# Down projections of a two-layer trunk: ten of 22 k-blocks in seven block products instead of eight

## The chip, the core and the metric

The kernel runs on one core of a Trainium2 chip. Its time is the device time of one execution in microseconds (us). Five engines work side by side, each through its own instructions in order: PE (TensorE, the matrix products; PEld is its weight loads), DVE (VectorE), ACT (ScalarE), POOL (GpSimd) and SP (SyncE), of which the last two issue transfers here. An engine stands still where its next instruction waits for another engine or for a transfer, and everything queued behind that instruction waits with it.

## What is computed

The reference runs two layers over 512 positions of 1024 channels. Each layer is a token mixer with a residual, then a gated feed-forward block with a residual:

```
u, v = split(h @ w_up)               # 1024 -> 2 x 2816
u = causal_dwconv(u, conv_w, conv_b)
y = (gelu(u) * v) @ w_down           # 2816 -> 1024
x = x + y
```

The change concerns the last product, with `w_down`, once in each layer. Cut into blocks of 128, it has 22 blocks of the summed dimension (k-blocks) and 8 blocks of outputs, and 512 positions as the moving side.

## The kernel before

**Three passes.** Every float32 operand is split into a high part (ACT copies it to the reduced type, `hi`) and a low part (DVE subtracts, `lo`). A product is three matmuls: high by high, high by low, low by high (`accumulate`, matmul in line 266; `seven_product`, line 538). Moving operands are split too (`mh`, `ml` and others, by `split`, lines 179 and 180).

**Seven in place of eight.** A product of a 2 by 2 arrangement of weight blocks with a 2 by 2 arrangement of operand blocks has eight block products. The kernel does seven, on sums and differences of the blocks, named p1 to p7. The two sides of the arrangement are a pair of output blocks, two groups of k-blocks, and the two halves of 256 positions (`lo_t`, `hi_t`), so these matmuls have 256 columns where plain ones have 512.

**Down projections** (inside `ffn`, lines 691 to 893). Of the 22 k-blocks 14 are plain (`NPLAIN`), in two weight blocks of seven (`DOWN_K`), for each of eight output blocks. The other eight go through the seven products, in two groups of four (`HK`), for four pairs p of output blocks. `UNIT` is the planned time of twelve half-width matmuls, one of the seven products; `MM` is that of one plain matmul. The order on PE is: output blocks 0 to 3 plain; then pair 0, block 4 plain; pair 1, block 5; pair 2, block 6; pair 3, block 7. In layer 1 the last plain block is done as two halves of positions (`down_half`), so that the final norm of the first half can run beside the second. Two of the seven products accumulate straight onto the plain sums of an even output block; the rest is put together by `keep` (line 799, ACT), `add_p5` (802), `add_left` (818) and `add_right` (823), which with `add_x` update `x` (815, 816), and `finish` squares `x` for the next norm (square on ACT 293, sum on DVE 294).

**Weights of a pair** (`seven_weights`, line 456). SP loads one part twice (462), POOL adds another by a summing transfer (466), SP loads the left part (470) and the right part (474). ACT and DVE then form the sums s2 (495) and s4 (501) and the high and low parts of pieces a1, s31p, s2 and a2 (484, 490). Plain weight blocks come through `fetch_steps` (216 load, 221 high, 225 low). The loads of left part, right part and plain blocks share three buffers of 1024 columns (`wp`, tag raw): a load waits in SP's queue until the low part of an earlier one has been taken.

**Order.** Inside `ffn` each step is put down with a planned time (`at`), and PE, DVE and ACT run their steps exactly in order of these times. The times set the order and nothing else; an engine that is early runs on, one that is late is late. SP and POOL are placed by the scheduler.

**Operands of the seven products** (`mix_m`, line 700). From the eight last gated blocks DVE forms four sums of 256 columns each per k-pair (716 to 719), and ACT and DVE split them. These run while PE does the plain blocks 0 to 3.

**The end** (`last`, line 1477 on, layer 1). After the first half of positions has its norm, `scale_first` (1560) scales it in groups of two channel blocks on DVE and SP sends each out (1561); the second half is transposed on PE, normed and sent as `res` (1554). Which step follows which matmul is set by a counter of matmuls (`after(14, ...)`, `after(25, ...)`).

Buffers: `big` has 41 tiles of 512 columns (`NBIG`), eight PSUM banks hold sums, and software-issued transfers have descriptor space at the start of the on-chip memory.

Of the kernel before, what the change touches and what calls it, by code (L numbers as in the profile page):

```python
# [7 lines left out]
F32 = mybir.dt.float32  # L8
# [6 lines left out]
P = 128  # L15
# [17 lines left out]
WPITCH = WBLK + 64  # L33
SKEW = 19
VG_SKEW = 48
NBIG = 41
NSIDE = 8
AHEAD = 1
H = T // 2
# [13 lines left out]
DOWN_SEVEN = ("p1", "p2", "p6", "p5", "p7", "p3", "p4")  # L53
PE_AT_FIRST = {"p1": 0, "p2": 1, "p3": 2, "p6": 3, "p5": 4, "p7": 7, "p4": 9}
PE_AT_LAST = {"p1": 0, "p2": 1, "p6": 3, "p5": 5, "p7": 6, "p3": 7, "p4": 8}
NPLAIN = NF - KD
DOWN_K = (7, 7)
DOWN_AT = (0, 7)
NDOWN = 6

COLS = {}
# [10 lines left out]


@with_exitstack
def trunk_kernel(ctx, tc, xT, cols, w_first, w_lead, w_ab, w_pool, w_abo, w_vg, w_qk, w_r, w_g2, w_go, w_up, w_dn, w_ds, out):
    nc = tc.nc
    V, S, G, PE = nc.vector, nc.scalar, nc.gpsimd, nc.tensor

# [351 lines left out]
    def at(t, fn):  # L430
        events.append((t, len(events), fn))
# [24 lines left out]
    def seven_weights(src, base, pool, sums, behind=False, lead=None, later=0.0, begin=(26.0, 20.0, 15.4, 9.7), early=0.0):  # L456
# [57 lines left out]
        when = (-6.75, -4.35, -2.7, -2.4, -1.65, -0.95, -0.3, 1.55, 1.5, 3.3)  # L514
        if pool == "up":
            when = (*when[:7], *((2.2, 1.5, 4.4) if lead is not None else (0.4, 1.5, 3.3)))
        if pool == "gla":
            when = (-6.75, -4.35, -2.1, -1.6, -0.9, -0.2, 0.5, 4.4, 1.5, 5.3)
        if lead is not None and lead < 2:
# [5 lines left out]

        return w

    def seven_product(w, b, ops, name, out, first, ts, only=None, low_last=False):
        if out not in b:
            b[out] = bank("st" + out)  # L530
        piece, side = LEFT[name]
        ks = [slice(side * QUARTER + k * P, side * QUARTER + (k + 1) * P) for k in range(HK)]
        h, lo = w[piece]
        ah, al = ops[name]()
        for i in range(3) if only is None else (only,):
            wt, a = ((h, ah), (lo, ah), (h, al))[i] if low_last else ((h, ah), (h, al), (lo, ah))[i]
            for k in range(HK):
                PE.matmul(  # L538
                    b[out][:, ts], wt[:, ks[k]], a[k],
                    start=first and i == 0 and k == 0, stop=i == 2 and k == HK - 1,  # L540
                    skip_group_check=True,
                )

# [72 lines left out]
    def ffn(l, acc, mixed, finish, ahead, halves_last=False):  # L616
# [83 lines left out]
        def mix_m(i, t):  # L700
            def low_part():
                if i % 2 == 0:
                    mixed_m["b1", i // 2] = slot(F32R, "bh"), slot(F32R, "bl")
                h, lo = [b[:, i % 2 * H : i % 2 * H + H] for b in mixed_m["b1", i // 2]]
                mixed_m["p1", i] = h, lo
                split(h, lo, ms[NPLAIN + i][:, lo_t])

            def right_part():
                h, lo = slot(F32R, "bh"), slot(F32R, "bl")
                split(h, lo, ms[NPLAIN + HK + i])  # L710
                mixed_m["p2", i] = h[:, lo_t], lo[:, lo_t]
                mixed_m["p3", i] = h[:, hi_t], lo[:, hi_t]

            def sums():
                m1, m2 = ms[NPLAIN + i], ms[NPLAIN + HK + i]
                V.tensor_tensor(m1[:, lo_t], m1[:, lo_t], m1[:, hi_t], ALU.subtract)
                V.tensor_tensor(m1[:, hi_t], m2[:, hi_t], m1[:, hi_t], ALU.subtract)
                V.tensor_tensor(m2[:, hi_t], m1[:, lo_t], m2[:, hi_t], ALU.add)
                V.tensor_tensor(m2[:, lo_t], m2[:, hi_t], m2[:, lo_t], ALU.subtract)

            def ta_part():
                split(xh[i], xl[i], ms[NPLAIN + i])
                mixed_m["p5", i] = xh[i][:, lo_t], xl[i][:, lo_t]
                mixed_m["p7", i] = xh[i][:, hi_t], xl[i][:, hi_t]

            def tb_part():
                h, lo = xh[HK + i], xl[HK + i]
                split(h, lo, ms[NPLAIN + HK + i])
                mixed_m["p6", i] = h[:, hi_t], lo[:, hi_t]
                mixed_m["p4", i] = h[:, lo_t], lo[:, lo_t]  # L730

            at(t, low_part)
            at(t + 0.4, right_part)
            at(t + 1.1, sums)
            at(t + 3.4, ta_part)
            at(t + 4.0, tb_part)

# [12 lines left out]
            base += PAIR + NORM * (j == 1)  # L750
        base -= PAIR
        at(base + 5.6, lambda: open_stage("dn", NDOWN))
        for t in (5.8, 6.6, 8.0, 10.3, 10.9, 11.5, 12.2, 14.5, 15.2, 16.4, 17.6, 18.3, 19.0, 20.6):
            at(base + t, split_m)
        for i in range(HK):
            mix_m(i, base + 22.0 + 6.2 * i)

        o, late, ops = {}, {}, {}

# [19 lines left out]

        def down_seven(p, base):  # L780
            w = seven_weights(w_ds[l, p], base, "dn", 2)
            b, q = {}, {}

            def product(name):
                if not ops:
                    for n in LEFT:
                        ops[n] = lambda n=n: ([mixed_m[n, i][0] for i in k1], [mixed_m[n, i][1] for i in k1])
# [6 lines left out]
                seven_product(w, b, ops, name, out, first, ts)  # L794

            def keep(tile, ts):
                if tile not in q:
                    q[tile] = slot(name=tile)
                S.activation(q[tile][:, ts], b["x"][:, lo_t], AF.Copy)

            def add_p5(tile):
                V.tensor_tensor(q[tile][:, hi_t], b["z"][:, lo_t], q[tile][:, hi_t], ALU.add)

            for n, name in enumerate(DOWN_SEVEN):
                at(base + n * UNIT, lambda name=name: product(name))
            at(base + 1 * UNIT + 0.1, lambda: keep("kk", lo_t))
            at(base + 3 * UNIT + 0.1, lambda: keep("kk", hi_t))
            at(base + 4 * UNIT + 0.2, lambda: add_p5("kk"))
            at(base + 5 * UNIT + 0.1, lambda: keep("uu", hi_t))
            at(base + 5 * UNIT + 0.6, lambda: add_p5("uu"))  # L810
            at(base + 7 * UNIT + 0.1, lambda: keep("uu", lo_t))
            return q

        def add_x(j, out, ts=slice(0, T)):
# [20 lines left out]
        blocks = list(down_blocks())  # L835
        parts = {}

        def plain_down(j):
            nonlocal t
            while blocks and (blocks[0][0] == j or (j == 0 and blocks[0][0] < 4)):  # L840
                jj, k0, kt = blocks.pop(0)
                first = t < base + 9.5 * UNIT
                block(t - 16.0, t - (9.3 if first else 6.0), t - (7.0 if first else 4.5))
                if halves_last and jj == KD - 1:
                    at(t, lambda a=(0, k0, kt): down_half(*a))
                    t += 1.5 * kt * MM
                else:
                    at(t, lambda a=(jj, k0, kt): down(*a))
                    t += 3 * kt * MM

        def sevens(p):
            nonlocal t
            parts[p] = down_seven(p, t)
            t += 7 * UNIT

        def done_left(p):
            at(t + 0.3, lambda: add_left(p))
            at(t + 2.3, lambda: finish(2 * p))

        def done_right(p, t):  # L860
            at(t, lambda: add_right(p))
            at(t + 2.4, lambda: finish(2 * p + 1))

        plain_down(0)
        for p in range(HK):
            sevens(p)
            done_left(p)
            if p < HK - 1:
                done_right(p, t + 3 * NPLAIN * MM + 0.3)
            elif halves_last:  # L870
                at(t + 0.5, lambda: early_right(p))
            else:
                for j in range(KD - 2):
                    at(t + 0.5 + 1.5 * j, lambda j=j: pre_split(j, "mix1"))
            plain_down(HK + p)
        if halves_last:
            at(t, lambda: add_x(KD - 1, o["half"][:, :H], lo_t))
            at(t, lambda: finish(KD - 1, 0))
# [602 lines left out]
    def last(j, half=None):  # L1481
# [33 lines left out]
        if half == 0:  # L1515
            S.activation(x[j][:, ts], x[j][:, ts], AF.Copy, scale=col("fin", j))

            def both():
                part(0, acc[:, ts])
                part(1, sq)  # L1520
                root()

            def spread():
                tokens.append(spread_small(y2, 2))
                scale_first((0, 2, 4))

            after(14, both)
            after(25, spread)
            return
        xf = slot(name="xf")[:, :256]  # L1530
        V.tensor_scalar(xf, x[j][:, ts], col("fin", j), None, ALU.mult)
        scale_first((6,))
        to = [[bank("to") for e in range(2)] for c in range(2)]

        def turn(k):
# [106 lines left out]
```

## Time and profile before

| What | us |
|---|---|
| median of 3 runs (lowest, highest) | 1000.76 (1000.57, 1000.95) |
| profiled execution, its own time | 1001.59 |
| its span, first to last instruction | 999.9 |
| PE busy in the span | 991.3 |
| DVE busy | 855.5 |
| ACT busy | 610.3 |
| down projections of layer 0, start to end on PE | 350.92 to 465.35 |
| down projections of layer 1, start to end on PE | 875.00 to 990.83 |

Times inside the profile count from the start of the span. The time of an execution is a little longer than its span, here by 1.69 us. A row of a group gives its line, engine, operation, output and inputs with shapes, then busy time, mean duration in ns and idle time before it with what ended that. The granted TensorE clock was 0.999 of full speed over the span.

### The profile page before, as it was taken

Reading aid. Unit: us, or ns where it says so; the run is one execution under the profiler, and the core shown is the slowest. Engines: PE = TensorE matmul, PEld = TensorE weight load, DVE = VectorE, ACT = ScalarE, POOL = GpSimd, SP = SyncE. Lnnn points to the kernel's source line nnn. Section 1 sums busy time; section 2 is a strip of 40 time slices with the busy share of each in tenths; the row PEclk is TensorE's granted clock in tenths of the full one; section 3 lists DMA queues with packets and bytes.
Section 4 is the critical chain, followed back from the end, with each engine's and each line's share of the span. In section 5 each row is a group of like instructions: output and inputs, shape, how many; then the busy total and the mean of one; then the engine's idle time right before and its main releaser. Section 6 shows DMA issues by size and latency. Waiting matters only on the chain.

```text
span 999.9 us, 18121 instructions
## 1 busy us (share of the span) xinstructions
PE 991.3 (99%) x7192; PEld 931.4 (93%) x7192; DVE 855.5 (86%) x1284; ACT 610.3 (61%) x995; POOL 85.8 (9%) x109
## 2 busy tenths in 40 slices
PE   9999999999999999999999999999999999999997
PEld 7888889999999988899999999889999999988897
DVE  7786689999999998668779789889999999997675
ACT  6432467676766764445776666667766666764543
POOL 0000111101101000002000000111110101000000
PEclk9999999999999999999999999999999999999999
DMA  7423666888777454527235453767778688455422
GB/s 252 128 99 106 167 139 165 212 213 195 186 196 192 138 129 130 141 88 188 98 95 143 116 123 109 200 156 177 210 205 215 163 211 184 139 122 144 129 87 85
DMA packets 65845, 154.39 MB, mean 154 GB/s; under 512 B 5505, under 2 KB 6913, under 8 KB 65761
## 3 DMA queue, kind: packets, MB, share of 16 engines
q1 hardware_dynamic: 47712, 118.76, 37.0%
q0 software_dynamic: 17760, 34.08, 20.5%
q8 instruction: 56, 0.92, 0.4%
q10 hardware_dynamic: 288, 0.40, 0.1%
q14 instruction: 29, 0.23, 0.1%
HBM read 148.50 MB, written 2.10 MB: 151 GB/s over the span
## 4 chain that ended last, share of the span: by engine, by line
PE 97%; DVE 1%; DMA 0%; issue 0%; ACT 0%; DVEq 0%; ACTq 0%
PE stx L538 32%; PE styz L538 19%; PE dn L266 15%; PE go L266 4%; PE abo L266 4%; PE pu L917 2%; PE pc L266 2%; PE dn L538 2%; PE pb L266 2%; PE px L266 2%; PE stz L538 2%; PE vg L1125 2%; PE vg L1126 1%; PE vg L1127 1%; PE o L1216 1%; PE stw L538 1%
## 5 line engine op out<-in xcount | busy, mean ns | idle before, releaser
L490 DVE TENSOR_TENSOR lo<-raw,hi 128x1024 fp32r<-128x1024 f32 x120 | 146.3, 1220 | 19.1 <-ACT hi L484 18.8
L484 ACT ACTIVATE hi<-raw 128x1024 fp32r<-128x1024 f32 x120 | 125.4, 1057 | 27.3 <-PE styz L538 10.8
L466 POOL DMA_DIRECT2D s<-in_w_up x44 | 53.1, 1206 | 477.8 <-ACT yh L179 96.5
L225 DVE TENSOR_TENSOR lo<-raw,hi 128x1024 fp32r<-128x1024 f32 (+3 forms) x69 | 78.8, 1144 | 8.6 <-ACT hi L221 8.0
L221 ACT ACTIVATE hi<-raw 128x1024 fp32r<-128x1024 f32 (+3 forms) x69 | 68.1, 990 | 25.6 <-PE px L266 9.1
L359 DVE SCALAR_TENSOR_TENSOR cacc<-u,colt,cacc 128x511 f32<-128x511 f32 x96 | 71.4, 744 | 2.6 <-ACT cacc L356 2.5
L490 DVE TENSOR_TENSOR lo<-s,hi 128x1024 fp32r<-128x1024 f32 x60 | 73.0, 1217 | 0.0
L356 ACT ACTIVATE cacc<-u,colt 128x512 f32<-128x512 f32 x48 | 39.2, 817 | 45.0 <-DVE u L660 41.5
L538 PE MATMUL stx<-th,hi 128*128 128x256 f32 x416 | 64.6, 277 | 0.0
L538 PE MATMUL stx<-tl,hi 128*128 128x256 f32 x416 | 64.1, 276 | 0.0
L538 PE MATMUL stx<-th,lo 128*128 128x256 f32 x416 | 64.1, 276 | 0.0
L484 ACT ACTIVATE hi<-s 128x1024 fp32r<-128x1024 f32 x60 | 63.3, 1055 | 0.8
L538 PE MATMUL styz<-xh,lo 128*128 128x256 f32 x400 | 61.8, 276 | 0.7 <-DVE lo L490 0.7
L538 PE MATMUL styz<-xh,hi 128*128 128x256 f32 x400 | 62.0, 277 | 0.0
L538 PE MATMUL styz<-xl,hi 128*128 128x256 f32 x400 | 61.6, 276 | 0.0
L266 PE MATMUL dn<-mh,hi 128*128 128x512 f32 (+1 forms) x238 | 56.8, 377 | 0.0
L484 ACT ACTIVATE sh<-raw 128x512 fp32r<-128x512 f32 x60 | 38.0, 633 | 30.5 <-DVE raw L495 30.5
L266 PE MATMUL dn<-mh,lo 128*128 128x512 f32 (+1 forms) x238 | 56.4, 376 | 0.0
L266 PE MATMUL dn<-ml,hi 128*128 128x512 f32 (+1 forms) x238 | 56.3, 376 | 0.0
L538 PEld LDWEIGHTS stx<-th,hi 128*128 128x128 f32 x416 | 54.9, 188 | 0.7 <-ACT k L645 0.3
L538 PEld LDWEIGHTS stx<-tl,hi 128*128 128x128 f32 x416 | 54.9, 188 | 0.0
L538 PEld LDWEIGHTS stx<-th,lo 128*128 128x128 f32 x416 | 54.9, 188 | 0.0
(356 smaller groups left out, 2557.8 us busy)
## 6 DMA issues: line engine op xcount, KB each, us to landing
s<-in_w_up SPq DMA_DIRECT2D x44, 512.0 KB, 6.3
s<-in_w_up POOLq DMA_DIRECT2D x44, 512.0 KB, 7.0
raw<-in_w_up SPq DMA_DIRECT2D x44, 512.0 KB, 6.0
raw<-in_w_dn SPq DMA_DIRECT2D x32, 448.0 KB, 3.4
raw<-in_w_up SPq DMA_DIRECT2D x44, 256.0 KB, 4.1
raw<-in_w_ab SPq DMA_DIRECT2D x12, 512.0 KB, 3.5
raw<-in_w_abo SPq DMA_DIRECT2D x8, 512.0 KB, 3.5
s<-in_w_ds SPq DMA_DIRECT2D x8, 512.0 KB, 5.3
```

Source lines behind the costliest of these rows:

```text
L221: S.activation(parts[0], raw, AF.Copy)
L225: V.tensor_tensor(parts[1], raw, f32(parts[0]), ALU.subtract)
L266: PE.matmul(out, w[:, k, :], a[k], start=first and i == 0 and k == 0, stop=last and i == 2 and k == n - 1, skip_group_check=loose,)
L356: S.activation(acc[0], u, AF.Identity, bias=col(bname, j), scale=col(wname, 2 * nj + j))
L359: V.scalar_tensor_tensor(a, u[:, : T - i], col(wname, (2 - i) * nj + j), a, ALU.mult, ALU.add)
L466: G.dma_start(w["s31"].rearrange("p (a n) -> p a n", a=2), part, accum_op=ALU.add)
L484: S.activation(h, src(), AF.Copy)
L490: V.tensor_tensor(lo, src(), f32(h), ALU.subtract)
L538: PE.matmul(b[out][:, ts], wt[:, ks[k]], a[k], start=first and i == 0 and k == 0, stop=i == 2 and k == HK - 1, skip_group_check=True,)
L917: PE.matmul(pus[g], parts[k][w][:, g * P : (g + 1) * P], a[k], start=k == 0 and i == 0, stop=k == KD - 1 and i == 2,)
L1125: PE.matmul(o[c][:, :n], xh[kk][:, cs], h[:, k, :], start=kk == 0, stop=False)
L1126: PE.matmul(o[c][:, :n], xl[kk][:, cs], h[:, k, :], start=False, stop=False)
```

## The change

Two more k-blocks go from the plain part to the seven products: 12 plain k-blocks in two weight blocks of six, and ten in two groups of five (`HD`). Each of the seven products thus has 15 matmuls instead of 12.

The fifth pair's weights come in a piece of their own, `w_de`, made ready by the new `extra_weights`: three transfers on SP into a buffer of the same three, three sums on DVE, one high and one low part of 896 columns. Its operands are mixed by a fifth `mix_m`. In the summing of a pair's weights the planned times of stage "dn" are new.

The order on PE is now: output blocks 0 to 4 plain, the first half (six k-blocks) of block 5, pair 0, second half of 5, pair 1, half of 6, pair 2, half of 6, pair 3, block 7. `done_left` comes 4.2 us later where a half block follows. `big` has four tiles more, and the descriptor space is set to 8192 bytes. In the end `scale_first` does two groups at its early place and two at its late one, where it did three and one.

```
-NBIG = 41
+NBIG = 45
-NPLAIN = NF - KD
-DOWN_K = (7, 7)
-DOWN_AT = (0, 7)
+HD = HK + 1
+NPLAIN = NF - 2 * HD
+DOWN_K = (6, 6)
+DOWN_AT = (0, 6)
+DOWN_UNIT = UNIT * HD / HK
+EXTRA_AT = {"a1": 0, "s31p": 2, "s2": 4, "a2": 5}
...
+        if pool == "dn":
+            when = (-4.0, -2.9, 0.1, -2.6, -2.0, -0.7, -0.1, 2.5, 1.4, 4.5)
...
+    def extra_weights(src, base):
+        e = {}
+        def load():
+            e["raw"] = wp.tile([P, WBLK], F32, tag="raw", name="raw_e")[:, : 7 * P]
+            nc.sync.dma_start(e["raw"][:, : 2 * P], src[:, : 2 * P])
+            e["r"] = e["raw"].rearrange("p (a n) -> p a n", n=P)
+            nc.sync.dma_start(e["r"][:, 2:4, :], src[:, None, 2 * P : 3 * P].broadcast_to([P, 2, P]))
+            nc.sync.dma_start(e["r"][:, 6, :], src[:, 3 * P :])
+        def sums():
+            r = e["r"]
+            V.tensor_tensor(r[:, 2:4, :], r[:, 2:4, :], r[:, 0:7:6, :], ALU.add)
+            V.scalar_tensor_tensor(r[:, 4, :], r[:, 3, :], -1.0, r[:, 0, :], ALU.mult, ALU.subtract)
+            V.tensor_tensor(r[:, 5, :], r[:, 1, :], r[:, 4, :], ALU.subtract)
+        def high():
+            e["hi"] = wsp.tile([P, WPITCH], F32R, tag="hi", name="hi_e")[:, SKEW : SKEW + 7 * P]
+            S.activation(e["hi"], e["raw"], AF.Copy)
+        def low():
+            e["lo"] = wsp.tile([P, WPITCH], F32R, tag="lo", name="lo_e")[:, SKEW : SKEW + 7 * P]
+            V.tensor_tensor(e["lo"], e["raw"], f32(e["hi"]), ALU.subtract)
+        at(base - 12.0, load)
+        at(base - 7.0, sums)
+        at(base - 3.0, high)
+        at(base - 1.7, low)
+        return e
...
-        for t in (5.8, 6.6, 8.0, 10.3, 10.9, 11.5, 12.2, 14.5, 15.2, 16.4, 17.6, 18.3, 19.0, 20.6):
+        for t in (5.8, 6.6, 8.0, 10.3, 10.9, 11.5, 14.5, 15.2, 16.4, 17.6, 18.3, 19.0):
             at(base + t, split_m)
-        for i in range(HK):
-            mix_m(i, base + 22.0 + 6.2 * i)
+        for i in range(HD):
+            mix_m(i, base + 20.5 + 6.2 * i)
...
-        def done_left(p):
-            at(t + 0.3, lambda: add_left(p))
-            at(t + 2.3, lambda: finish(2 * p))
+        def done_left(p, late=0.0):
+            at(t + late + 0.3, lambda: add_left(p))
+            at(t + late + 2.3, lambda: finish(2 * p))
...
         plain_down(0)
-        for p in range(HK):
+        plain_down(4)
+        plain_down(5, 1)
+        for p, (j, n) in enumerate(((5, 1), (6, 1), (6, 1), (7, 2))):
             sevens(p)
-            done_left(p)
+            done_left(p, 4.2 if n == 1 else 0.0)
             if p < HK - 1:
-                done_right(p, t + 3 * NPLAIN * MM + 0.3)
+                done_right(p, t + 1.5 * n * NPLAIN * MM + 3.2)
             elif halves_last:
                 at(t + 0.5, lambda: early_right(p))
             else:
-                for j in range(KD - 2):
-                    at(t + 0.5 + 1.5 * j, lambda j=j: pre_split(j, "mix1"))
-            plain_down(HK + p)
+                for i in range(KD - 2):
+                    at(t + 0.5 + 1.3 * i, lambda i=i: pre_split(i, "mix1"))
+            plain_down(j, n)
...
-                scale_first((0, 2, 4))
+                scale_first((0, 2))
...
-        scale_first((6,))
+        scale_first((4, 6))
...
-    nc = _bacc.Bacc("TRN2", target_bir_lowering=False, num_devices=1)
+    nc = _bacc.Bacc("TRN2", target_bir_lowering=False, num_devices=1, dynamic_dma_scratch_size=8192)
```

More of the change, by code (lines that the diff above doesn't have):

```diff
@@ L55 @@
 PE_AT_LAST = {"p1": 0, "p2": 1, "p6": 3, "p5": 5, "p7": 6, "p3": 7, "p4": 8}
-NPLAIN = NF - KD
-DOWN_K = (7, 7)
-DOWN_AT = (0, 7)
+HD = HK + 1
[4 more added lines that the diff above has]
+EXTRA_AT = {"a1": 0, "s31p": 2, "s2": 4, "a2": 5}
+DOWN_LEFT = [NPLAIN + i for i in range(HK)] + [NF - 2]
+DOWN_RIGHT = [NPLAIN + HK + i for i in range(HK)] + [NF - 1]
 NDOWN = 6
@@ L74, in trunk_kernel @@
 @with_exitstack
-def trunk_kernel(ctx, tc, xT, cols, w_first, w_lead, w_ab, w_pool, w_abo, w_vg, w_qk, w_r, w_g2, w_go, w_up, w_dn, w_ds, out):
+def trunk_kernel(ctx, tc, xT, cols, w_first, w_lead, w_ab, w_pool, w_abo, w_vg, w_qk, w_r, w_g2, w_go, w_up, w_dn, w_ds, w_de, out):
     nc = tc.nc
@@ L526, in seven_weights, with seven_product @@
         return w
-    def seven_product(w, b, ops, name, out, first, ts, only=None, low_last=False):
+    def extra_weights(src, base):
[22 more added lines that the diff above has]
+        return e
+    def seven_product(w, b, ops, name, out, first, ts, only=None, low_last=False, extra=None):
         if out not in b:
@@ L532, in seven_product @@
         ks = [slice(side * QUARTER + k * P, side * QUARTER + (k + 1) * P) for k in range(HK)]
-        h, lo = w[piece]
+        h, lo = [[t[:, c] for c in ks] for t in w[piece]]
+        if extra:
+            c = (EXTRA_AT[piece] + side) * P
+            h, lo = h + [extra["hi"][:, c : c + P]], lo + [extra["lo"][:, c : c + P]]
         ah, al = ops[name]()
@@ L536, in seven_product @@
             wt, a = ((h, ah), (lo, ah), (h, al))[i] if low_last else ((h, ah), (h, al), (lo, ah))[i]
-            for k in range(HK):
+            for k in range(len(a)):
                 PE.matmul(
-                    b[out][:, ts], wt[:, ks[k]], a[k],
-                    start=first and i == 0 and k == 0, stop=i == 2 and k == HK - 1,
+                    b[out][:, ts], wt[k], a[k],
+                    start=first and i == 0 and k == 0, stop=i == 2 and k == len(a) - 1,
                     skip_group_check=True,
@@ L705, in low_part @@
                 mixed_m["p1", i] = h, lo
-                split(h, lo, ms[NPLAIN + i][:, lo_t])
+                split(h, lo, ms[DOWN_LEFT[i]][:, lo_t])
             def right_part():
                 h, lo = slot(F32R, "bh"), slot(F32R, "bl")
-                split(h, lo, ms[NPLAIN + HK + i])
+                split(h, lo, ms[DOWN_RIGHT[i]])
                 mixed_m["p2", i] = h[:, lo_t], lo[:, lo_t]
@@ L714, in sums @@
             def sums():
-                m1, m2 = ms[NPLAIN + i], ms[NPLAIN + HK + i]
+                m1, m2 = ms[DOWN_LEFT[i]], ms[DOWN_RIGHT[i]]
                 V.tensor_tensor(m1[:, lo_t], m1[:, lo_t], m1[:, hi_t], ALU.subtract)
@@ L721, in ta_part @@
             def ta_part():
-                split(xh[i], xl[i], ms[NPLAIN + i])
-                mixed_m["p5", i] = xh[i][:, lo_t], xl[i][:, lo_t]
-                mixed_m["p7", i] = xh[i][:, hi_t], xl[i][:, hi_t]
+                h, lo = (xh[i], xl[i]) if i < HK else (slot(F32R, "eh"), slot(F32R, "el"))
+                split(h, lo, ms[DOWN_LEFT[i]])
+                mixed_m["p5", i] = h[:, lo_t], lo[:, lo_t]
+                mixed_m["p7", i] = h[:, hi_t], lo[:, hi_t]
             def tb_part():
-                h, lo = xh[HK + i], xl[HK + i]
-                split(h, lo, ms[NPLAIN + HK + i])
+                h, lo = (xh[HK + i], xl[HK + i]) if i < HK else (slot(F32R, "eh"), slot(F32R, "el"))
+                split(h, lo, ms[DOWN_RIGHT[i]])
                 mixed_m["p6", i] = h[:, hi_t], lo[:, hi_t]
@@ L781, in down_seven @@
             w = seven_weights(w_ds[l, p], base, "dn", 2)
+            extra = extra_weights(w_de[l, p], base)
             b, q = {}, {}
@@ L786, in product @@
                     for n in LEFT:
-                        ops[n] = lambda n=n: ([mixed_m[n, i][0] for i in k1], [mixed_m[n, i][1] for i in k1])
+                        ops[n] = lambda n=n: [[mixed_m[n, i][e] for i in range(HD)] for e in range(2)]
                 b["yz"] = o.get(2 * p)
@@ L793, in product @@
                 }[name]
-                seven_product(w, b, ops, name, out, first, ts)
+                seven_product(w, b, ops, name, out, first, ts, extra=extra)
             def keep(tile, ts):
@@ L804, in down_seven @@
             for n, name in enumerate(DOWN_SEVEN):
[L805 to L811, printed above, removed]
+                at(base + n * DOWN_UNIT, lambda name=name: product(name))
+            at(base + 1 * DOWN_UNIT + 0.1, lambda: keep("kk", lo_t))
+            at(base + 3 * DOWN_UNIT + 0.1, lambda: keep("kk", hi_t))
+            at(base + 4 * DOWN_UNIT + 0.2, lambda: add_p5("kk"))
+            at(base + 5 * DOWN_UNIT + 0.1, lambda: keep("uu", hi_t))
+            at(base + 5 * DOWN_UNIT + 0.6, lambda: add_p5("uu"))
+            at(base + 7 * DOWN_UNIT + 0.1, lambda: keep("uu", lo_t))
             return q
@@ L836, in ffn, with plain_down @@
         parts = {}
-        def plain_down(j):
+        def plain_down(j, n=None):
             nonlocal t
-            while blocks and (blocks[0][0] == j or (j == 0 and blocks[0][0] < 4)):
+            while blocks and n != 0 and (blocks[0][0] == j or (j == 0 and blocks[0][0] < 4)):
                 jj, k0, kt = blocks.pop(0)
+                n = n and n - 1
                 first = t < base + 9.5 * UNIT
@@ L853, in sevens @@
             parts[p] = down_seven(p, t)
-            t += 7 * UNIT
-        def done_left(p):
-            at(t + 0.3, lambda: add_left(p))
-            at(t + 2.3, lambda: finish(2 * p))
+            t += 7 * DOWN_UNIT
+        def done_left(p, late=0.0):
+            at(t + late + 0.3, lambda: add_left(p))
+            at(t + late + 2.3, lambda: finish(2 * p))
         def done_right(p, t):
@@ L1623 @@
         "w_ds": np.stack([
-            _blocks(a["ffn_w_down"][l][NPLAIN * P :], P).reshape(KD // 2, 2, P, D).transpose(0, 2, 1, 3).reshape(KD // 2, P, 2 * D)
+            _blocks(a["ffn_w_down"][l][NPLAIN * P : NPLAIN * P + D], P).reshape(HK, 2, P, D).transpose(0, 2, 1, 3).reshape(HK, P, 2 * D)
+            for l in range(2)
+        ]),
+        "w_de": np.stack([
+            _blocks(a["ffn_w_down"][l][NPLAIN * P + D :], P).reshape(HK, 2, P, 2 * P).transpose(0, 2, 1, 3).reshape(HK, P, 4 * P)
             for l in range(2)
```

## The prediction

> **What bounds the kernel now.** I read the busy times first, then who PE waited for, then the chain of work that ended last, then the stretches of the down projections one by one.
>
> ```profile
> span 999.9 us, 18121 instructions
> PE 991.3 (99%) x7192; PEld 931.4 (93%) x7192; DVE 855.5 (86%) x1284; ACT 610.3 (61%) x995; POOL 85.8 (9%) x109
> ```
>
> ```profile
> PE warm L162 <- DVE half L168: 1.1, 1, 1.1
> PE styz L538 <- DVE lo L490: 0.7, 1, 0.7
> PE pu L917 <- ACT xh L911: 0.3, 1, 0.3
> PE vg L1125 <- DVE z L1073: 0.2, 1, 0.2
> ```
>
> PE is busy 991.3 of 999.9 us, and all its recorded waits for another engine come to 2.3 us, none on a line of the down projections (their `dn`, `stx`, `stz` rows are missing here). So matmul time taken out there is taken out of the span, as long as nothing new makes PE wait. The chain in layer 0:
>
> ```profile
> 350.92 38.10 PE dn L266 x168
> 389.03 1.37 PE stx L538 x12
> ...
> 398.56 9.54 PE dn L266 x42
> 408.11 1.37 PE stx L538 x12
> ...
> 455.80 9.54 PE dn L266 x42
> 465.35 0.12 PE vg L1125
> ```
>
> Each stretch begins where the one before ends. A plain matmul is paced at 38.10/168 = 0.2268 us. The 84 half-width matmuls of a pair run from 389.03 to 398.56: 9.53/84 = 0.1135 us each, just half. The engines beside PE in these stretches (us, then for each engine busy time and instructions):
>
> ```profile
> 350.90:389.03 38.13, 38.13 (x171) 31.56 (x170) 35.27 (x60) 22.27 (x37) 1.49 (x2) 1.00 0.43 111
> 408.10:417.60 9.50, 9.50 (x86) 9.50 (x85) 5.94 (x8) 4.31 (x7) 1.20 (x1) 1.00 0.50 153
> 417.60:427.20 9.60, 9.60 (x45) 7.94 (x44) 7.77 (x12) 3.55 (x5) 0.00 (x0) 1.00 0.57 143
> 455.80:465.30 9.50, 9.50 (x44) 7.84 (x43) 8.82 (x13) 6.86 (x11) 0.39 (x1) 1.00 0.54 145
> ```
>
> The third busy time is DVE's: 35.27 of 38.13 us (92%) in the plain stretch, and 5.94 + 7.77 = 13.71 of 19.10 us (72%) in a period of one pair and one plain block. PE did not wait in either. DVE is the second limit, and the one to check.
>
> **The change part by part.**
>
> *Matmuls.* Per layer two plain k-blocks go: 2 x 3 passes x 8 output blocks = 48 x 0.2268 = 10.89 us. Three matmuls join each of seven products of four pairs: 84 x 0.1135 = 9.53 us. Net 1.36 us per layer, 2.72 us in all. All of it lies on the chain, since PE stands nowhere in these stretches.
>
> A page speaks against this: the Trainium skill, TensorE: Matmul & The Clock Gate, section Back-to-back issue gap, gives a warm matmul a fixed 2.5 ns beside its columns, 109.2 ns for 256 columns and 215.8 for 512. By it 168 added cost 18.34 us, 96 removed give back 20.72, and the saving is 2.37 us, an estimate from that page. Here the rows show no fixed part, and the measured pace decides.
>
> *Weights on DVE and ACT.* The rows of DVE between 408.1 and 427.2 us, one period:
>
> ```profile
> L490 DVE TENSOR_TENSOR lo<-raw,hi 128x1024 fp32r<-128x1024 f32 x2 | 2.4, 1222 | 0.3 <-ACT hi L484 0.3
> L225 DVE TENSOR_TENSOR lo<-raw,hi 128x896 fp32r<-128x896 f32 x2 | 2.2, 1088 | 0.4 <-ACT hi L221 0.4
> L294 DVE TENSOR_TENSOR acc<-acc,sq 128x512 f32<-128x512 f32 x2 | 1.4, 692 | 3.0 <-ACT sq L293 3.0
> L816 DVE TENSOR_TENSOR xall<-kk,xall 128x512 f32<-128x512 f32 x1 | 0.7, 691 | 0.0
> L802 DVE TENSOR_TENSOR uu<-stz,uu 128x256 f32<-128x256 f32 x1 | 0.4, 425 | 0.8 <-ACT uu L799 0.8
> ```
>
> A period is now a pair of 105 x 0.1135 = 11.92 us and a half block of 18 x 0.2268 = 4.08: 16.00 us. Of DVE's 13.71 us one low part of 896 columns goes (1.09), the other shrinks to 768 (1.09 x 768/896 = 0.93, so 0.16 less), the fifth pair's low part of 896 comes (1.09), and its sums of 256, 128 and 128 columns, at most the 256-column 0.42 each, 1.26. That makes 14.81 of 16.00 us, 93%. ACT had 4.31 + 3.55 = 7.86 us; in place of two high parts of 896 columns it has one of 896 and one of 768, so it stays under 8. I cost both at nothing, because 93% is what DVE carried in the plain stretch with PE never waiting; if the cover is gone, it is priced below as the second rival.
>
> *Lead.* The low part of a1 is planned 2.9 us ahead of its pair and takes 1.22; p1 needs it in its third pass, 10 x 0.1135 = 1.14 us in. So a step that DVE does 2.8 us late costs PE nothing. s2, s31p and a2 have at least as much.
>
> *Loads.* Per period four loads pass through the three raw buffers. SP's waits in the whole run (total, times, longest), one issue of a load on SP, and the sizes and median times from issue to landing:
>
> ```profile
> SPq L474 <- DVE raw L501: 269.0, 49, 8.9
> SPq L216 <- DVE lo L225: 190.3, 45, 9.2
> ```
>
> ```profile
> 413.29 0.33 SPq L470 DMA_DIRECT2D raw<-in_w_ds  x1
> ```
>
> ```profile
> raw<-in_w_dn SPq DMA_DIRECT2D x32, 448.0 KB, 3.4
> raw<-in_w_ds SPq DMA_DIRECT2D x8, 512.0 KB, 3.7
> s<-in_w_ds POOLq DMA_DIRECT2D x8, 512.0 KB, 7.1
> raw<-in_w_ds SPq DMA_DIRECT2D x8, 256.0 KB, 3.4
> ```
>
> From planned load to the end of the last reader by the planned times and rows above: left part 15.4 - 0.1 + 0.7 = 16.0 us, extra 12 - 1.7 + 1.1 = 11.4, right 9.7 + 4.5 + 1.2 = 15.4, half block 16 - 4.5 + 0.9 = 12.4; together 55.2 against 3 x 16.00 = 48.0 available. (Before: 15.8 + 14.2 + 2 x 12.6 = 55.2 against 57.3.) So loads start late, 7.2 us in sum per period. Their spare time takes it: the half block has 10 us from load to its high part and needs 3.4, the left part 11.4 and needs 3.7. The extra piece is three issues in a row on SP; behind them stand the right part, the next pair's twofold load (and behind that POOL's sum) and the next half block. If it lands in 3.4 us behind three issues of 0.4, it is there at -7.4; from landing to its low part DVE and ACT need 1.26 + 0.9 + 1.1 = 3.3 us, and PE wants it at about +1.6. So it may be 5.7 us late. I take nothing for it; bounds are 0 and a wait of 7.2 - 5.7 = 1.5 us in each of six pairs (pair 0 of each layer stands after a long plain stretch), 9 us.
>
> *Mixing.* The fifth `mix_m` gives DVE five operations of 256 columns (0.42, as line 802) and three of 512 (0.69, as line 816), 4.2 us; two splits less take away 1.4, and the plain stretch before pair 0 grows from 38.1 to 198 x 0.2268 = 44.9 us. With three more low parts (2.8), the shrinking of seven (-1.1) and the extra piece (2.35), DVE has 42.1 of 44.9 us there: 94%, as before. Nothing.
>
> *Moved sums.* `add_left` runs 4.2 us later, behind the next pair's start, `add_right` inside that pair; who waits for them is the norm, not PE. Bank by bank: six plain sums and the two of a pair fill all eight PSUM banks, so the next pair's first product needs ACT's last `keep`, planned 4.0 us earlier. Nothing. The last block of layer 0, with six splits for the next stage, has 8.82 us of DVE work (window row) where 8.2 are left, so the next stage starts 0.6 us late on DVE; its third weight group is what reads them, over 4 us in. Nothing.
>
> *More tiles, smaller descriptor space.* POOL's sums take 7.1 us each and come once per period, planned 17 us ahead of use; even two in a row would fit. Four more tiles can only take waits away. I take 0; bounds are -0.7 (PE's one wait on a low part) and +1.2 (one issue of a sum on POOL, window row, held up once where it counts).
>
> *The end.* PE's last matmuls, then DVE and ACT, then the last stretch as a whole (last number: GB/s):
>
> ```profile
> 988.85 1.98 PE dn L266 x17
> ```
>
> ```profile
> 988.89 1.88 DVE L1560 TENSOR_TENSOR xall<-xall,bc 128x512 f32<-128x512 f32 x3 [0.99 <-PE bc L332]
> 990.87 0.43 DVE L815 TENSOR_TENSOR dn<-dn,rs 128x256 f32<-128x256 f32 x1
> 992.07 0.68 DVE L1560 TENSOR_TENSOR xall<-xall,bc 128x512 f32<-128x512 f32 x1
> 992.91 0.26 ACT L1510 ACTIVATE y<-ss,eps_t 128x2 f32<-128x2 f32 x1 [0.70 <-PE ss L1502]
> 993.21 0.16 DVE L1511 SCALAR_TENSOR_TENSOR t<-ss,y 128x2 f32<-128x2 f32 x1 [0.46 <-ACT y L1510]
> ```
>
> ```profile
> 990.80:999.90 9.10, 2.79 (x25) 2.46 (x23) 3.69 (x9) 1.95 (x4) 0.00 (x0) 0.85 0.62 221
> ```
>
> At the counter's 25 there were 42 - 25 = 17 matmuls left; now 36 - 25 = 11, 1.25 us. Two scalings (1.28) just fit ahead of line 815. Late, two scalings take 992.07 to 993.36 on the old clock, and line 1511 wanted DVE at 993.21: 0.15 us on the path. The second late transfer is issued about 0.6 us later than the one before, ahead of the last `res`: 0, at most one transfer of 256 KB at the 221 GB/s of this stretch, 1.2 us. I take 0.2 in all.
>
> **Sum.** -2.72 + 0.2 = -2.5 us. The profiled execution (1001.59, span 999.9) would take 999.1; it stands 0.8 above the median of the runs, so the median goes from 1000.76 to 998.3.
>
> **The rivals.**
>
> *A wait on the late loads.* For it: 55.2 us of buffer time in 48.0. Against it: each load has more spare than its share, and SP already waited 5 us at a time (269.0/49) without PE noticing. A wait of 0.2 to 0.7 us in each of six pairs gives 999.5 to 1002.5, at 0.4 about 1000.7: the gain is spent, no measurable change.
>
> *DVE in order becomes the bound: slower.* In the old period DVE stood 19.10 - 13.71 = 5.4 us, mostly for ACT (3.0 for squares, 0.8 for `uu`); now 1.2 us are free. If w us of these waits stay, three periods in a row make DVE 3 x (w - 1.2) late, of which the lead takes 2.8. With all 5.4 that is 9.8 us a layer, 998.3 + 19.6 = 1018. Break-even is 1.25 a layer, w = 2.6; it is slower by 0.2% from w = 2.9. Against it: a DVE that is late finds ACT done, so the waits shrink as it falls behind. If w is 3.4, 3.8 us a layer, it is 1006.
>
> *The half-width matmuls cost more than half.* Then the change doesn't do what it says. The rows give 0.1135 against 0.2268/2 = 0.1134: worth 168 x 0.0001, nothing. The page's fixed part would leave 998.6.
>
> **How the numbers follow.** 0.2% (2.0 us) is about what a measurement of this kernel tells from no change: 998.8 and 1002.8 are the borders. Forecast, no new wait beyond half a microsecond: 0.54, with the fixed part (0.01) 0.55 faster. Gain mostly spent on late loads or a short DVE backlog: 0.25, same. DVE bound or long waits on loads: 0.20, slower. The forecast's own range is 997.6 (a wait gone elsewhere) to 998.8; the range for 8 in 10 goes on through the second case and the foot of the third, to 1003.5.
>
> **What would show it.** PE matmuls in number 7192 + 72 = 7264; a pair at 11.92 us and 16.00 us from pair to pair; layer 0's down projections 113.1 us in place of 114.4; no row of PE waiting on lines of the seven products. Wrong if PE waits for the low or high parts of the extra piece (loads) or of a1, s2 or a2 with DVE without idle time (order), or if the end behind the last plain matmul grows by more than 0.5 us.

## The result, and the profile after

The changed kernel takes 998.88 us (median of 13 runs, 997.56 to 1001.42) against 1001.11 us before in the runs beside it (13 runs, 1000.57 to 1003.77). The ratio is 0.9974 with a 95% interval of 0.9965 to 0.9982, that is 1.8 to 3.5 us less; the medians differ by 2.2. Forecast were 2.5 us, a ratio of 0.9975.

The busy times and PE's waits of the changed kernel, from its page and from the view of who waited for whom:

```profile
span 996.3 us, 18359 instructions
PE 987.6 (99%) x7258; PEld 931.7 (94%) x7258; DVE 868.7 (87%) x1328; ACT 614.9 (62%) x1007; POOL 86.0 (9%) x109
```

```profile
PE warm L167 <- DVE half L173: 1.1, 1, 1.1
PE styz L579 <- DVE lo L495: 0.7, 1, 0.7
PE pu L963 <- ACT xh L957: 0.4, 1, 0.4
PE vg L1171 <- DVE z L1119: 0.2, 1, 0.2
```

PE's waits are the same four as before, none of them in the down projections; DVE has 13 us more to do. The page counts 7258 matmuls, 66 more than before, where 72 more were expected (see below). The line numbers have moved: 538 is now 579, 266 is 271, 490 is 495. The chain of layer 0 (start, length):

```profile
350.05 44.90 PE dn L271 x198
394.95 1.71 PE stx L579 x15
...
406.87 4.11 PE dn L271 x18
410.97 1.71 PE stx L579 x15
...
454.93 8.19 PE dn L271 x36
```

From 350.05 to 454.93 + 8.19 = 463.12 are 113.07 us, where there were 114.43 (350.92 to 465.35). That is the 1.36 us of the sum. In layer 1, from the first plain matmul to the first transpose behind the last one, it was 875.00 to 990.67 and is 872.75 to 987.06: 115.67 became 114.31, again 1.36. Its first and its last block in the chain of the changed kernel:

```profile
872.75 44.90 PE dn L271 x198
...
977.63 5.67 PE dn L271 x50
```

The span fell by 3.6 us, more than the 2.72. The other 0.87 us is gone before the down projections begin (350.05 for 350.92). Most of it stands in the first products of the kernel, which PE begins while their operands still arrive; the chain has it in one row of before, then one of after:

```profile
5.23 23.03 PE pu L917 x96
```

```profile
5.31 22.41 PE pu L963 x96
```

The change touches no instruction there. Whether its room in memory does is the first experiment.

The windows of two periods and of the plain stretch, for the third busy time, DVE's:

```profile
350.05:394.95 44.90, 44.90 (x200) 37.17 (x200) 42.24 (x74) 25.61 (x43) 2.41 (x2) 1.00 0.46 121
410.97:426.99 16.02, 16.02 (x126) 15.30 (x125) 13.69 (x21) 7.53 (x12) 1.20 (x1) 1.00 0.64 160
426.99:443.01 16.02, 16.02 (x126) 15.30 (x125) 14.11 (x22) 7.59 (x12) 0.00 (x0) 1.00 0.31 96
```

42.24 of 44.90 and 13.69 to 14.11 of 16.02: the shares that were forecast (42.1; at most 14.81), with PE never short. Layer 1's second and third period have 13.76 and 14.20.

### The profile page after: what moved, and what is told of

Same layout as the page of the kernel before. It is cut to its first block, busy times and chain, and to the rows that moved or that the text cites. A ratio compares the mean times of both kernels' runs of the same rounds, so it can differ in the third digit from the quotient of the medians.

```text
span 996.3 us, 18359 instructions
## 1 busy us (share of the span) xinstructions
PE 987.6 (99%) x7258; PEld 931.7 (94%) x7258; DVE 868.7 (87%) x1328; ACT 614.9 (62%) x1007; POOL 86.0 (9%) x109
## 4 chain that ended last, share of the span: by engine, by line
PE 97%; DVE 2%; DMA 0%; issue 0%; ACT 0%; DVEq 0%; ACTq 0%
PE stx L579 33%; PE styz L579 19%; PE dn L271 13%; PE go L271 4%; PE abo L271 4%; PE dn L579 3%; PE stz L579 2%; PE pu L963 2%; PE pc L271 2%; PE pb L271 2%; PE px L271 2%; PE vg L1171 2%; PE vg L1173 1%; PE vg L1172 1%; PE o L1262 1%; PE stw L579 1%
## 5 line engine op out<-in xcount | busy, mean ns | idle before, releaser
L495 DVE TENSOR_TENSOR lo<-raw,hi 128x1024 fp32r<-128x1024 f32 x120 | 146.2, 1219 | 16.4 <-ACT hi L489 16.2
L226 ACT ACTIVATE hi<-raw 128x1024 fp32r<-128x1024 f32 (+3 forms) x69 | 64.7, 940 | 25.1 <-PE px L271 9.1
L230 DVE TENSOR_TENSOR lo<-raw,hi 128x1024 fp32r<-128x1024 f32 (+3 forms) x69 | 74.9, 1088 | 5.7 <-ACT hi L226 4.8
L579 PEld LDWEIGHTS styz<-xh,lo 128*128 128x128 f32 x400 | 52.8, 188 | 0.9 <-DVE lo L495 0.9
L579 PEld LDWEIGHTS styz<-xh,hi 128*128 128x128 f32 x400 | 52.9, 188 | 0.0
L579 PEld LDWEIGHTS styz<-xl,hi 128*128 128x128 f32 x400 | 52.8, 188 | 0.0
```

The source lines that it names most:

```text
L226: S.activation(parts[0], raw, AF.Copy)
L230: V.tensor_tensor(parts[1], raw, f32(parts[0]), ALU.subtract)
L495: V.tensor_tensor(lo, src(), f32(h), ALU.subtract)
L579: PE.matmul(b[out][:, ts], wt[k], a[k], start=first and i == 0 and k == 0, stop=i == 2 and k == len(a) - 1, skip_group_check=True,)
```

## Experiments

Theory: the gain is PE's saved matmul time, with DVE and the loads hidden and some 3 us (lead) and 5.7 us (loads) to spare. Rivals: part of the gain is room in memory; DVE's order, or the loads, already stand at the edge. Where a kernel ran once, I go by its two stretches of down projections, which the chain gives to hundredths: layer 0's as above, 113.07 us in the changed kernel, and layer 1's from the first plain matmul to the first one of the last output block, there 872.75 to 977.63, 104.88 us.

### Room in memory alone

```
(on the kernel before)
-NBIG = 41
+NBIG = 45
-    nc = _bacc.Bacc("TRN2", target_bir_lowering=False, num_devices=1)
+    nc = _bacc.Bacc("TRN2", target_bir_lowering=False, num_devices=1, dynamic_dma_scratch_size=8192)
```

> The kernel before with 45 tiles and 8192 bytes of descriptor space, nothing else. If the gain is matmul time alone (2.7 us), this changes nothing: within 0.2% of before, PE waits as before. If part of the gain is room in memory or the shorter start seen in the profile of the changed kernel (layer 0's down projections begin at 350.05 in place of 350.92), this kernel takes 0.5 to 1 us less than before, and its down projections of layer 0 begin near 350.1.

Measured: 1001.55 us against 1001.62 before, ratio 0.9998 (0.9989 to 1.0007). Its chain:

```profile
350.42 38.10 PE dn L266 x168
```

So the room is worth nothing by itself. In this one profile the down projections begin at 350.42, between the two others. Over the kernels below, which all share the front of the program, they begin anywhere from 349.66 to 350.94. So I take the 0.87 us for the spread of the start, and for no part of the effect; each kernel has one profile only, and the cause of the spread is not shown.

### More work for DVE: 2.5 and 5 us per pair

```
(on the changed kernel, in down_seven; 8, and in a second kernel 16)
+            def load_dve():
+                for _ in range(8):
+                    V.tensor_tensor(ones, ones, ones, ALU.mult)
+            at(base - 6.5, load_dve)
```

> The changed kernel with eight idle DVE operations of 128 columns (about 0.3 us each, 2.5 us) ahead of each pair's low parts, 6.5 us before the pair. DVE then has 13.7 + 2.5 = 16.2 of 16.0 us in a period. If the spare time and the lead of some 3 us hide it, PE waits nowhere in the down projections and a period stays at 16.02 us. If DVE in its order already bounds the period, each added microsecond shows: some 2 us in each of six periods, 12 us in all.

> The same with sixteen operations, 5 us per pair: 18.8 us of DVE work in a period of 16.0. Lateness of 2.8 us per period over three periods less a lead of 3 to 5 us: PE waits 3 to 5 us in each layer, 6 to 10 us in all, first at pair 2 or 3. If DVE had no lead at all it would be 17 us; if DVE's order waits vanish when it is late, under 4.

Measured, one run each: 1003.58 and 1027.04 us. Layer 0's down projections take 115.23 and 126.76 us; with eight operations layer 1's stretch takes 108.67. PE's waits with eight operations:

```profile
PE stx L579 <- DVE lo_e L558: 1.5, 2, 0.9
...
PE stx L579 <- ACT kk L847: 1.0, 2, 0.5
...
PE stx L579 <- ACT uu L847: 0.6, 1, 0.6
PE stx L579 <- DVE lo L495: 0.4, 1, 0.4
```

Both are worse than forecast: with eight operations 2.2 us in layer 0 and 3.8 in layer 1 where none was expected, with sixteen 13.7 in layer 0 where 3 to 5 were. The rows above make 3.5 of these 6.0 us with eight operations; in the rest PE counts as busy (113.98 us in layer 0, for work of 113.07). The extra piece's low part (`lo_e`) is what PE waits for most. With eight operations two of them in a row are 426.59 - 409.16 = 17.4 us apart, the next 18.1. Adding 2.5 us of work to 13.7 to 14.1 should give 16.2 to 16.6. So something takes 1 to 2 us per period beside DVE's work, and it doesn't shrink as DVE falls behind.

### Less work for PE

This kernel leaves out the fifth matmul of each pass of the seven products, and so computes with eight k-blocks where ten belong; the weights and operands of the fifth are still made.

```
(on the changed kernel, in seven_product and in the operands' lists)
-        if extra:
+        if extra and not extra:
...
-    ... for i in range(HD)] for e in range(2)]
+    ... for i in range(HK)] for e in range(2)]
```

> The changed kernel with the fifth matmul of each pass of the seven products left out (its weights and operands are still made; ten k-blocks become eight in the result). 168 half-width matmuls less, 19.1 us if PE alone bounds: 979.8 against 998.9. The period falls to 13.6 us, DVE's work in it is 13.7 to 14.1, so up to 0.5 us per period may come back, 3 us: 980 to 983. If DVE bounded the changed kernel already, little of the 19 us would show.

Measured: 985.66 us, ratio to before 0.9841 (0.9828 to 0.9855); 13.2 us less than the changed kernel, where PE's share was 19.1. So some 5.9 us come back as waits, twice the most I expected. Layer 0's down projections take 106.39 us, where 113.07 - 9.53 = 103.54 is what PE needs. The chain of waits of this kernel, one round of it (start, length):

```profile
413.81 1.23 DVE lo L495
415.06 0.33 SPq L541
...
415.91 2.40 DMA raw_e<-in_w_de
...
418.43 0.44 DVE raw_e L548
...
419.84 1.13 DVE lo L495
...
421.58 1.00 DVE lo_e L558
...
429.67 1.23 DVE lo L495
430.92 0.33 SPq L541
```

Here the loop can be seen. The low part of a2 (413.81) is the last reader of a raw buffer. When it ends, SP may issue the extra piece's load (415.06). DVE's next step but a few is the first sum of that piece (line 548), so DVE stands until it lands. Then come DVE's low parts and sums in order up to the low part of a2 of the next pair (429.67), which lets the next extra load go. One round is 429.67 - 413.81 = 15.9 us, of which DVE stands about 1.6 us for the load; the next is 15.6 (the low part of a2 starts again at 445.23). In the changed kernel a period of PE is 16.02. The loop also gives what the added work cost: 15.6 + 2.5 is the 18.1 us seen with eight operations, and 15.6 + 5 is 20.6, where with sixteen PE's wait for a low part ends at 435.06 in one pair and at 455.76 in the next, 20.7 us later.

### The same with a fourth raw buffer

```
(on the kernel just shown)
-    wp = ctx.enter_context(tc.tile_pool(name="wp", bufs=3))
+    wp = ctx.enter_context(tc.tile_pool(name="wp", bufs=4))
...
-    dynamic_dma_scratch_size=8192
+    dynamic_dma_scratch_size=4096
```

> The kernel without the fifth matmuls (eight k-blocks in the result in place of ten, as before), now with four raw buffers in place of three and the descriptor space at 4096 bytes to make room. Without the fourth buffer the time from one low part of the extra piece to the next was 15.4 to 15.6 us, against 13.6 us of PE work. If that is a loop through the buffers (extra load waits for the low part of a2, the rest of DVE's order waits for the extra load), a fourth buffer opens it: the loop falls to 13.7 to 14.2 us, layer 0's down projections take 104 to 105 us in place of 106.4, the time falls by 2.5 to 5 us to 981 to 983. If DVE's own work and its waits for ACT make the 15.5 us, nothing changes: 985.7.

Measured: 980.78 us, ratio 0.9796 (0.978 to 0.9813): 4.9 us less than with three buffers. Its chain:

```profile
350.46 44.90 PE dn L271 x198
404.90 4.10 PE dn L271 x18
418.54 4.10 PE dn L271 x18
...
445.82 8.18 PE dn L271 x36
454.00 0.13 PE vg L1171
```

That is 103.54 us, to the hundredth what PE needs, with a period of 13.64 us. (Layer 1, where ACT has more to do, still loses 1.7 us of 95.4, with one wait of 1.2 for ACT.) The rows of DVE and of SP show the loop open: the extra load (422.29) is issued before the low part of a2 (428.02), and DVE's step before the sums runs into them without standing.

```profile
422.29 0.33 SPq L541 DMA_DIRECT2D raw_e<-in_w_de  x1
```

```profile
428.02 1.22 DVE L495 TENSOR_TENSOR lo<-raw,hi 128x1024 fp32r<-128x1024 f32 x1
...
430.09 0.95 DVE L230 TENSOR_TENSOR lo<-raw,hi 128x768 fp32r<-128x768 f32 x1
430.96 0.42 DVE L548 TENSOR_TENSOR raw_e<-raw_e 128x256 f32<-128x256 f32 x1
```

So the second limit is this loop through three buffers; the last experiment shows the same for the changed kernel. DVE's sum of work comes behind it: here DVE runs from one low part of a2 (413.78) to the next (428.02) without standing, 14.2 us for a period of 13.64; that PE doesn't wait for it in layer 0 I put down to DVE's lead.

### A later extra load

```
(on the changed kernel, in extra_weights)
-            nc.sync.dma_start(e["raw"][:, : 2 * P], src[:, : 2 * P])
+            for _ in range(3):
+                nc.sync.dma_start(e["raw"][:, : 2 * P], src[:, : 2 * P])
```

> The changed kernel with the first transfer of the extra piece done three times in a row, each waiting for the one before to land: it lands some 4.5 us later. By the prediction's account, 5.7 us of lateness are free: PE waits nowhere. By the loop through the buffers (15.5 us of 16.0) nearly all of it shows: the loop becomes 20 us, 4 us too long in three periods less a lead of 3 us, PE waits 8 to 9 us in each layer, 17 in all.

Measured, one run: 1033.83 us; layer 0's down projections take 131.60 us, 18.5 more.

```profile
PE stx L580 <- ACT hi_e L555: 16.7, 6, 6.6
PE stx L580 <- DVE lo_e L559: 2.5, 4, 0.7
```

And three links of its chain in a row, the first period's transfers of the extra piece:

```profile
400.13 4.48 DMA raw_e<-in_w_de
404.63 2.12 DMA raw_e<-in_w_de
406.77 6.12 DMA raw_e<-in_w_de
```

The load came later than the 4.5 us that were meant. Single transfers took 4 to 8 us to land (4.48 and 6.12 above, 7.79 in the next period) where others took about 2, for a reason that I did not follow up. In the first period the piece is there at 412.89, some 10 us later than in the changed kernel, where line 548 starts at 403.08 without a wait; PE stood 2.9 us for it, so about 7 us were hidden. In the second period the set takes 12.2 us from its first issue (424.85) to the end of the last transfer, where the changed kernel has the piece 3.6 us after the issue; of these 8.6 us PE stood 6.6. So the 5.7 us that I had counted free are there once, and not in each period. With transfers that late the run doesn't test the size that the loop was reckoned to give (17 us in all, where 35 were lost); part of it is also PE's clock, which fell behind the long waits (last section).

### The left sum without its delay

```
-            done_left(p, 4.2 if n == 1 else 0.0)
+            done_left(p)
```

> The changed kernel with the sum of the left output planned at once after its pair in place of 4.2 us later, so that its three operations (2.1 us) come ahead of the next pair's a1 and extra low parts. The low part of the extra piece was ready 1.7 us ahead of the pair and is wanted 1.6 us into it: 3.3 us of lead less 2.1 leaves 1.2, so PE waits nowhere and the time stays. If the loop is tight enough for the move to lengthen it, PE waits from pair 2 on, up to 2 us in each layer.

Measured, one run: 1001.19 us; layer 0's down projections take 113.80 us, 0.73 more, and layer 1's stretch 874.01 to 980.77, 106.76 us, 1.88 more.

```profile
PE stx L579 <- DVE lo_e L558: 1.8, 3, 0.7
```

The first pairs are undisturbed, later ones wait for the extra piece's low part. The delay of `done_left` is no detail: without it 2.6 us are lost, about as much as the matmuls save.

### The end as before

```
-                scale_first((0, 2))
+                scale_first((0, 2, 4))
...
-        scale_first((4, 6))
+        scale_first((6,))
```

> The changed kernel with three scalings early and one late, as before the change. The last matmul ends at about 1.3 us after the early scalings begin, three take 1.9: line 858's last use starts 0.55 us later behind PE, the late one is 0.05 shorter on the path: from the last matmul to the end of the span 9.6 us in place of 9.1. If DVE is not on that path, 9.1 stays.

Measured, one run, span 997.1 us. DVE in time order, first this kernel, then the changed one:

```profile
986.30 1.88 DVE L1606 TENSOR_TENSOR xall<-xall,bc 128x512 f32<-128x512 f32 x3 [0.99 <-PE bc L337]
988.10 0.43 DVE L858 TENSOR_TENSOR dn<-dn,rs 128x256 f32<-128x256 f32 x1
```

```profile
985.96 1.28 DVE L1606 TENSOR_TENSOR xall<-xall,bc 128x512 f32<-128x512 f32 x2 [0.99 <-PE bc L337]
987.26 0.43 DVE L858 TENSOR_TENSOR dn<-dn,rs 128x256 f32<-128x256 f32 x1
```

Line 858 starts 0.70 us after PE's first transpose (987.40) instead of 0.20 (987.06). From that transpose to the start of line 1597, which makes the last result, it is 3.68 us, against 3.24 in the changed kernel and 3.19 before (line 1551 there); to the end of the span 9.7, 9.2 and 9.2. As expected, moving one scaling behind saves about 0.5 us on this path; the whole time of a single run can't show it.

### A fourth buffer in the changed kernel, without and with DVE's extra work

```
(the four buffers of above, on the changed kernel; and on the one with eight operations)
```

> The changed kernel with four raw buffers and 4096 bytes of descriptor space. PE waits nowhere in its down projections, so there is nothing to win: they stay at 113.1 us per layer and the time within 0.2% of the changed kernel's 998.9. If POOL's transfers need the descriptor space, PE waits appear beside them and the time grows.

> The changed kernel with eight idle DVE operations per pair, as before, and four raw buffers. With three, PE waited 3.5 us and layer 0's down projections took 115.2 us. If the loop through the buffers is the second limit and not DVE's sum of work (16.2 of 16.0 us), the fourth buffer takes nearly all of that away: 113.1 to 113.6 us. If DVE's sum is the limit, 115 us stays.

Measured: 998.3 us without (5 runs, ratio to before 0.9964, 0.995 to 0.9978), not told apart from the changed kernel's 0.9974, with the same stretches of 113.07 and 104.88 us; and 999.25 us (one run) with the eight operations. The chain of the latter, where 115.23 us became 464.01 - 350.94 = 113.07:

```profile
350.94 44.90 PE dn L271 x198
...
455.82 8.19 PE dn L271 x36
464.01 0.13 PE vg L1176
```

With the fourth buffer 2.5 us more of DVE work per pair cost nothing in layer 0 and 0.35 us in layer 1 (873.61 to 978.84), where three buffers lost 2.2 and 3.8. The changed kernel doesn't get faster by the buffer, since PE is never short in it.

## Why the prediction was right

**Matmuls.** 2.72 us were reckoned, 1.36 a layer; both layers show 1.36. The pace of a half-width matmul is just half that of a full one in this kernel too, and nothing shows of the fixed 2.5 ns per matmul of the Trainium skill, TensorE: Matmul & The Clock Gate, section Back-to-back issue gap: by it a layer would have gained 1.19, an estimate from that figure. The Trainium skill gives that gap there for a single matmul by itself and not for a stream, so it spoke less against the forecast than the prediction made of it. The expected number of matmuls was wrong, though not their time: layer 0 has 36 more, but layer 1 only 30, since its last plain block is done in halves and loses 12 half matmuls (84 became 72) where the count took 6 whole ones.

**The end.** 0.2 us were taken as a loss; from the first transpose to the end of the span it is 9.2 us as before. Line 858 follows PE's first transpose by 0.20 us as before, since the two early scalings just fit; the late ones cost 0.05 on the path (3.24 us for 3.19), and the later transfer nothing that the span shows. The bound of 1.2 us for it was far too wide. That the forecast of 2.5 lies nearer to the 2.2 of the medians than 2.7 does is luck: the traces give 2.7, and the interval holds all three.

**DVE's work.** 93% of a period was forecast, with 1.26 us for the extra sums; they take 1.00, and the period has 13.69 to 14.20 us over both layers (85 to 89%). In the plain stretch 42.1 were forecast and 42.24 are there. Layer 0's last block has 7.29 us of DVE work (window 454.93 to 463.10), not 8.82. PE waited nowhere in the down projections.

**The moved sums** were put at nothing, which holds only for the place that they have: the delay of the left one is worth 0.73 us in layer 0 and 1.88 in layer 1.

**The margin** is where the reasoning was weak, though it didn't cost the result. I counted two spares apart: DVE's lead of 2.8 us, and 5.7 us for the extra load. They are one. The load waits for a buffer that DVE frees, and DVE waits in its order for the load. In the changed kernel the extra load, planned 12 us ahead, is issued 10.0 us ahead of one pair and 9.4 ahead of the next:

```profile
416.99 0.33 SPq L541 DMA_DIRECT2D raw_e<-in_w_de  x1
...
433.61 0.33 SPq L541 DMA_DIRECT2D raw_e<-in_w_de  x1
```

These are 16.62 us apart, against a period of 16.02, but the load doesn't slip further: between the extra piece's low part and the low part of a2 DVE has one operation more from here on (line 299, 0.69 us), which moves it once. The rows that end the next period on DVE:

```profile
440.20 1.09 DVE L558 TENSOR_TENSOR lo_e<-raw_e,hi_e 128x896 fp32r<-128x896 f32 x1 [0.26 <-ACT hi_e L554]
...
448.39 1.22 DVE L495 TENSOR_TENSOR lo<-raw,hi 128x1024 fp32r<-128x1024 f32 x1
```

The low part of a2 before that starts at 432.37, 16.02 us earlier, and the extra piece's low part follows the one before by 16.02 too (424.18). PE sets this pace: DVE stands 0.26 us for ACT's `hi_e`, which comes in ACT's order behind a `keep` that waits for PE. So the loop closes 0.26 us inside the period here, and DVE's wait for `hi_e` ahead of the last two pairs of either layer is never longer than 0.46 us. The forecast of rival two, that a late DVE finds others done and its waits shrink, fell: its wait for the extra load stays (1.3 us a period with eight operations added, 1.4 to 1.5 in the changed kernel, layer 0). The break-even of 2.6 us of waits was reckoned without the loop, and 2.5 us of added work were enough to lose 6.0 us in two layers.

**The chance of slower** (0.20) was then not too high: the kernel stands within half a microsecond per period of it.

## What to carry to other kernels

Where PE has no waits, a change is worth the matmul time that it saves, and rows of the same shape give that to hundredths; the work is in finding how near the next limit is. Don't add up spare time load by load and engine by engine: if a load waits for a buffer that an in-order engine frees, and that engine waits for the load, then follow one round through and compare its length with the period. Two cheap runs show the distance: add idle work to the second engine, and take work from the first.

## What the runs showed of the hardware

PE's clock follows its waits, which the kernels before and after hardly show (granted clock 0.999 and 0.998 over the span). In the kernel with the late load, windows of layer 0 (the third number from the end is the granted clock):

```profile
430.00:455.00 25.00, 18.42 (x122) 17.61 (x121) 14.02 (x21) 7.97 (x12) 0.00 (x0) 0.80 0.37 97
462.00:467.41 5.41, 5.39 (x33) 5.40 (x34) 5.31 (x8) 2.42 (x4) 0.00 (x0) 0.68 0.51 145
```

In the second row one product of 15 matmuls takes 3.12 us (462.40 to 465.52) instead of 1.70; the waits just ahead of it were 1.54 and 0.63 us long. In windows of 2 us of the same trace the granted clock is 0.50 from 416 to 418, behind a wait of 2.94 us, and 0.50 from 436 to 444, in and behind the wait of 6.58. The Trainium skill, TensorE: Matmul & The Clock Gate, section HAM oscillation — how this bites in real kernels, says that gaps of more than some 3.4 us between matmuls halve the clock for a time. The halving agrees with these rows, the length doesn't: shorter waits did it here. Nor is there one length in these runs: with sixteen operations added, waits of 1.43 and 0.88 us in a row left the clock at 1.00 (415 to 425). So a wait can cost more than itself, and how long it must be stays open.

The descriptor space for POOL's summing transfers, 8192 bytes in the changed kernel and 4096 in the one with four buffers, made no difference that could be measured (ratios 0.9998 for 8192 bytes and four more tiles alone, 0.9964 for 4096 and a fourth buffer beside the changed kernel's 0.9974).
